# Weight parts at shifted starts in their buffers, and eleven raw tiles in place of twelve, in a one-core fp32 decoder layer

## Chip, cores and metric

The kernel runs on one core of a Trainium2 chip. The metric is the device time of one execution in microseconds (us). Three runs of the kernel before took 1511.15 to 1511.68 us, median 1511.59 us.

## The reference

One conditioned decoder layer on 256 tokens of width 2048, all in fp32, and a final norm:

```python
mod = silu(c) @ w_ada + b_ada          # shift1, scale1, gate1, shift2, scale2, gate2
h   = rms_norm(x, g1) * (1 + scale1) + shift1
p   = h @ w_in                         # retention q,k,v,g | HGRN2 q,f,i,g | gate A | gate B
yA  = (LN_head(retention(rope(q), rope(k), v)) * silu(g)) @ w_ret_o
yB  = (RMS_head(hgrn2(silu(q), f, i)) * silu(g)) @ w_hg_o
x   = x + gate1 * ((sigmoid(gA) * yA + sigmoid(gB) * yB) @ w_out)
h2  = rms_norm(x, g2) * (1 + scale2) + shift2
a,b = split(causal_conv3(h2 @ w_up))   # 2 x 5632 columns
x   = x + gate2 * ((silu(a) * b) @ w_down)
out = rms_norm(x, g_final)
```

What costs is the weights: w_ada (2048 x 12288), w_in (2048 x 12288), w_up (2048 x 11264), w_down (5632 x 2048), and three smaller ones. Each is read once.

## The kernel before

Every large product is made of three products of parts. A weight w is split into a high part wh (w rounded to float32r, the form in which TensorE takes fp32 data in one pass) and a low part wl = w - wh; an activation likewise into a high and a low half, which lie side by side in one block (columns 0 to T and T to 2T, T = 256). The sum is hi x wh + lo x wh + hi x wl.

The weights come in groups of 512 output columns (G). `pieces` walks a group two k-tiles (2 x 128 rows of the weight) at a time. For each such piece `load` starts one transfer of 512 KB from SyncE's queue (SP) into a raw tile, `upper` has ScalarE copy raw into wh (line L169), and `rest` has VectorE subtract wh from raw into wl (L174). Raw has 12 slots, wh and wl 4 each, all in the pool `wp`. A slot of raw is sized for the largest user, the 1025 columns of the modulation dots (`ada_dot`), which stream w_ada through the same raw tiles and reduce it on VectorE (L458). Behind `wp` in SBUF lies the pool `sb`, with the activations in blocks of 4096 bytes (tag k4).

`products` and `up_group` consume the pieces. There are two orientations:

- `mm_rows` (L198, L199 with wh, L203 with wl): the activation is stationary and the weight part is the moving operand, 512 columns wide. It serves part of the input projection, the gates A and B (wab, 8 groups), w_hg_o (whg, 4), w_ret_o (wret, 4), w_out (wout, 4) and w_down (wdown, 4 groups of 44 k-tiles).
- `mm_cols` (L214, L215, L218), `wide_group` with `mm_wide` (L225, L228; the retention q and k, wk, 4 groups) and `up_group` (L1125, L1127; w_up, 22 groups): the weight part is stationary, 128 columns at a time, and the activation moves, 256 or 512 columns wide.

The stages follow each other: norm and modulation with the first stage of the input projection (wa), wk, wab, whg, wret, wout, then the up-projection with its convolution, then w_down and the final norm. Attention work and the modulation of later stages are woven in by `pump`, which runs generators against a budget per piece. Weight loads and conversions are held in program order by `pin` while `self.ordered` is set; elsewhere a scheduler orders them. In the last group of wout and of wdown the weights are multiplied by the gate first (L165). SP's queue is in order, so a load that waits for a free raw slot holds back those behind it.

Of the kernel before, what the change touches and what calls it, by code (L numbers as in the profile page):

```python
# [12 lines left out]
F32 = mybir.dt.float32  # L13
F32R = mybir.dt.float32r
# [5 lines left out]
P = 128  # L20
# [3 lines left out]
KT = D // P  # L24
# [4 lines left out]
FT = FF // P  # L29
G = 512  # L30
# [5 lines left out]
LAG = 1  # L36
NOSYNC = mybir.DependencyInfo(mybir.DependencyClass.NoSync, mybir.DependencyReason.DATA)
SMALL = 70

C_RQ, C_RK, C_RV, C_RG, C_HQ, C_HF, C_HI, C_HG = (i * W1 for i in range(8))  # L40
C_GA, C_GB = 8 * W1, 8 * W1 + D
# [16 lines left out]
class Kernel:  # L58
# [95 lines left out]

    def load(self, src, m, w):
        self.n += 1
        raw = self.wp.tile([P, m, w], F32, name=f"raw_{self.n}", tag="raw", bufs=12)
        self.pin(self.nc.sync.dma_start(out=raw, in_=src))
        return raw

    def upper(self, src, m, w, gain=None):

        raw = self.load(src, m, w)
        if gain is not None:
            self.pin(self.nc.vector.tensor_tensor(raw, raw, gain[:, None, :].to_broadcast([P, m, w]), ALU.mult))  # L165
        self.n += 1
        wh = self.wp.tile([P, m, w], F32R, name=f"wh_{self.n}", tag="wh", bufs=4)
        wl = self.wp.tile([P, m, w], F32R, name=f"wl_{self.n}", tag="wl", bufs=4)
        self.pin(self.nc.scalar.activation(wh, raw, AF.Copy))  # L169
        return raw, wh, wl  # L170

# [3 lines left out]
        self.pin(self.last)  # L175
        return wh, wl

    def pieces(self, src, kts, gain=None):

        uppers = []  # L180
        for k in range(0, kts, 2):
            m = min(2, kts - k)

            while len(uppers) <= k // 2 + (gain is not None) and 2 * len(uppers) < kts:
                at = 2 * len(uppers)
                z = min(2, kts - at)
                uppers.append(self.upper(src[:, at : at + z, :], z, G, gain))
            wh, wl = self.rest(uppers[k // 2])
            uppers[k // 2] = None
            yield [(k + j, wh[:, j, :], wl[:, j, :]) for j in range(m)]  # L190
# [36 lines left out]
            for z in (pair, pair + 1):  # L227
                nc.tensor.matmul(ps[z][:, :T], lhsT=wl[:, z * P : (z + 1) * P], rhs=act[:, :T], start=False, stop=last and i == len(items) - 1)  # L228

    def wide_group(self, src, act):  # L230

        nc = self.nc
        pgs = [self.pg(), self.pg()]
        ps = pgs[0][:2] + pgs[1][:2]
        steps = list(range(0, KT, 4))
        pieces = self.pieces(src, KT)
        for k in steps:
            items = [(act(kt), wh, wl) for _ in range(2) for kt, wh, wl in next(pieces)]
            for pair in (0, 2):
                self.mm_wide(ps, items, k == 0, k == steps[-1], pair)  # L240
                self.pump()
        out = self.blk([P, 4, T], name="p")
        for pair in (0, 2):
            dst = out[:, pair : pair + 2, :]
            z = pgs[pair // 2][2]
            nc.scalar.activation(dst, z[:, :, T:], AF.Copy)
            nc.vector.tensor_tensor(dst, dst, z[:, :, :T], ALU.add)  # L247
        return out

    def products(self, mm, ps, src, act, k0, kts, hold=0, first=True, last=True, gain=None):  # L250

        held = []
        for step in self.pieces(src[:, k0 : k0 + kts, :], kts, gain):
            items = [(act(k0 + kt), wh, wl) for kt, wh, wl in step]
            kt = step[0][0]
            if kt >= kts - hold:
                held += items
            else:
                mm(ps, items, first and kt == 0, last and kt + len(step) == kts)
            self.pump(len(step) / 2)  # L260
        for t in range(NT if held else 0):
            mm(ps, held, hold == kts, True, [t])
        return ps

    def rows(self, src, act, k0=0, kts=KT, ps=None):
        return self.parts(self.products(self.mm_rows, ps or self.pg(), src, act, k0, kts), True)

    def put_split(self, dst, src):

# [524 lines left out]
    def run(self):  # L794
        nc, a = self.nc, self.a
# [42 lines left out]
        ps = [self.po2(), self.po2(), self.pg(), self.pg()][:FIRST]  # L838
# [33 lines left out]
        g = FIRST  # L872
        att, gates = [], {}

        def begin(kind, hb, *ins):
            att.append(self.start(kind(hb, *ins, gates)))
# [43 lines left out]
        self.pace(1, 68.0, 96)  # L920
        sgb, sga = [], []
        for hb in range(2):
            begin(self.retention, hb, *[self.wide_group(a["wk"][2 * hb + i], act) for i in range(2)], v.pop(0))

        og = [[], []]

# [5 lines left out]
        att.append(self.start(gating(1)))  # L932
        for j in range(8):
            gt = self.blk([P, NT, G], name="gt")
            for at, z in self.rows(a["wab"][j], act):
                nc.scalar.activation(gt[:, at, :], z, AF.Sigmoid)
            (sgb if j < 4 else sga).append(gt)
        hT = None
        self.finish(*att)
        self.pace(1, 44.0, 60)  # L940
        for j in range(4):
            for at, z in self.rows(a["whg"][j], lambda k: og[0][k // 2][:, k % 2, :], 0, 8):
                nc.vector.tensor_tensor(sgb[j][:, at, :], sgb[j][:, at, :], z, ALU.mult)
        og[0] = None
        mT = []
# [9 lines left out]
        self.pace(0, 10.0, 16)  # L955
        merges = []
        for j in range(4):
            for at, z in self.rows(a["wret"][j], lambda k: og[1][k // 2][:, k % 2, :], 0, 8):
                nc.vector.tensor_tensor(sga[j][:, at, :], sga[j][:, at, :], z, ALU.mult)
            nc.vector.tensor_tensor(sga[j], sga[j], sgb[j], ALU.add)  # L960
            merges.append(self.start(merged(sga[j])))
# [13 lines left out]
        for j in range(4):  # L975
            last = j == 3
            x1.append(self.load_rows(j))
            if not last:
                g = self.row(self.gate["gate1"], j, "g1")
            if j == 2:  # L980
                g3 = self.row(self.gate["gate1"], 3, "g1")
            elif last:
                g = g3
            ps = self.products(self.mm_rows, self.po2() if last else self.pg(), a["wout"][j], actm, 0, KT, hold=4 * last, gain=g if last else None)
            if last:
                g = None
                self.finish(ada2)
                up = self.pieces(a["wup"][0], KT)
                up = chain([next(up), next(up)], up)
                self.ordered = True  # L990
            if last:
                break
            for t in range(NT):
                self.residual(x1[j], ps, g, ss, j, t)
            if j == 2:
                part = self.row_part(ss)
# [61 lines left out]
        for i in range(FT // 2):  # L1058
            if i == 2:
                g2 = self.start(self.gate_cols("gate2"), 1)  # L1060
                self.pace(1, 38.0, 144)
            if i % 2 == 0:
                gT.append(self.blk([P, 4, T], name="gT"))
            self.up_group(i, act2, gT, up if i == 0 else self.pieces(a["wup"][i], KT), pu if i == 0 else None)
        h2T = None
        self.down(gT, x1, g2)

# [80 lines left out]
    def down(self, gT, x1, g2):  # L1148
        nc, a = self.nc, self.a
        gs = []  # L1150
        sqs = []

        def act(kt):
            if kt == 2 * len(gs):
                z = self.blk([P, 2, 2 * T], F32R, name="gs")
                self.put_split(z, gT[kt // 4][:, kt % 4 : kt % 4 + 2, :])
                gs.append(z)
            return gs[kt // 2][:, kt % 2, :]

        self.finish(g2)  # L1160
        self.gate_row("gate2")
        self.sqrt_table()
        ss = self.small([P, NT, 4], name="ss", bufs=2)
        for j in range(4):
            last = j == 3
            if not last:
                g = self.row(self.gate["gate2"], j, "g2")
            if j == 2:
                g3 = self.row(self.gate["gate2"], 3, "g2")
            elif last:  # L1170
                g = g3
            f = self.row(a["gf"], j, "gf")
            ps = self.products(self.mm_rows, (self.pg, self.po2)[j % 2](), a["wdown"][j], act, 0, FT, hold=8 * last, gain=g if last else None)
            if last:
                g = None
            if j == 0:
                gT = None
            if last:
                self.ordered = True
            for t in range(NT):  # L1180
                self.residual(x1[j], ps, g, ss, j, t)
                if last:

                    y = self.s2([P, G], name="y")
                    self.pin(nc.vector.tensor_tensor(y, x1[j][:, t, :], f, ALU.mult))
                    self.finished([z[:, t, :] for z in x1[:3]] + [y], self.row_rstd(ss, part, t), t)
                else:
                    self.pin(nc.vector.tensor_tensor(x1[j][:, t, :], x1[j][:, t, :], f, ALU.mult))
            if j == 2:
                part = self.row_part(ss)  # L1190
# [101 lines left out]
```

## Time and profile before

| | |
|---|---|
| median of three runs | 1511.59 us |
| the profiled execution | 1511.24 us |
| its span, first to last instruction | 1509.5 us |
| TensorE matmuls | 1493.7 us busy, 8466 |
| weight loads (beside the matmuls) | 1275.5 us |
| VectorE | 1211.9 us |
| ScalarE | 841.7 us |
| read from HBM | 382.11 MB, 255 GB/s over the span |

Busy is the time in which at least one instruction of the engine ran. PE is TensorE's matmuls, PEld its weight loads, DVE VectorE, ACT ScalarE, SP the queue that starts the transfers; an engine name with q is its sequencer, which waits and issues. Matmuls are pipelined: the length of one in the trace is longer than the distance to the next, and the distance is what a stream of them costs. "<-" names what ended a wait.

### The profile page before, as it was taken

How to read it: one execution, taken by the hardware profiler on the slowest of the kernel's cores; microseconds unless marked ns; L12 is line 12 of the kernel's file. 1: busy time of each engine (PE TensorE's matmuls, PEld its weight loads, DVE VectorE, ACT ScalarE, POOL GpSimd, SP SyncE). 2: the span in 40 equal slices, each digit the busy share in tenths (PEclk: the TensorE clock that was granted, in tenths of full speed). 3: DMA queues.
4: the chain of work that ended last, by engine and by line, in shares of the span. 5: the costliest groups of instructions: out<-in, count | busy, mean ns of one | idle time of the engine just before them, and what ended most of it. 6: DMA issues, size and time to landing. Idle time of an engine off the chain costs nothing.

```text
span 1509.5 us, 22703 instructions
## 1 busy us (share of the span) xinstructions
PE 1493.7 (99%) x8466; PEld 1275.5 (84%) x8466; DVE 1211.9 (80%) x1647; ACT 841.7 (56%) x1210; POOL 4.0 (0%) x8
## 2 busy tenths in 40 slices
PE   8999999999999999999999999999999999999997
PEld 6889899888888888888888888888888888888886
DVE  7899997998999877898977778777777769455784
ACT  6745456767775644455466555555555658344342
POOL 0000000000000000000000000000000000000000
PEclk9999999999999999999999999999999999999999
DMA  9999997777887899989847777777777666667651
GB/s 373 376 347 336 321 320 257 265 248 274 281 278 262 285 302 326 318 290 361 298 132 242 229 233 230 230 231 238 229 239 231 216 193 204 197 206 212 183 171 56
DMA packets 110994, 385.71 MB, mean 256 GB/s; under 512 B 12802, under 2 KB 13346, under 8 KB 110884
## 3 DMA queue, kind: packets, MB, share of 16 engines
q1 hardware_dynamic: 110016, 383.14, 76.7%
q8 instruction: 66, 1.08, 0.3%
q10 hardware_dynamic: 868, 1.13, 0.2%
q14 instruction: 44, 0.36, 0.1%
HBM read 382.11 MB, written 2.11 MB: 255 GB/s over the span
## 4 chain that ended last, share of the span: by engine, by line
PE 93%; DVE 3%; ACT 1%; issue 1%; DMA 1%; SPq 0%; DVEq 0%; ACTq 0%
PE pg L198 13%; PE pg L203 13%; PE pg L199 13%; PE po L1125 11%; PE pg L1125 10%; PE po L1127 5%; PE pg L1127 5%; PE pg L225 4%; PE po L198 3%; PE po L203 3%; PE po L199 3%; PE pg L228 2%; DVE wl L174 1%; DVE raw L458 1%; PE po L218 1%
## 5 line engine op out<-in xcount | busy, mean ns | idle before, releaser
L174 DVE TENSOR_TENSOR wl<-raw,wh 128x1024 fp32r<-128x1024 f32 (+1 forms) x536 | 633.1, 1191 | 233.6 <-ACT wh L169 230.6
L169 ACT ACTIVATE wh<-raw 128x1024 fp32r<-128x1024 f32 (+1 forms) x536 | 547.9, 1033 | 482.5 <-PE pg L199 167.0
L458 DVE SCALAR_TENSOR_TENSOR raw<-raw,sc 128x1024 f32<-128x1024 f32 x192 | 233.8, 1222 | 0.1
L1125 PE MATMUL po<-h2T,wh 128*128 128x512 f32 x704 | 221.1, 395 | 0.0
L1125 PE MATMUL pg<-h2T,wh 128*128 128x512 f32 x688 | 216.4, 396 | 0.0
L198 PE MATMUL pg<-wh,hT 128*128 128x512 f32 x512 | 202.1, 395 | 0.9 <-DVE p L830 0.6
L199 PE MATMUL pg<-wh,hT 128*128 128x512 f32 x512 | 199.8, 390 | 0.0
L1127 PEld LDWEIGHTS po<-h2T,wl 128*128 128x128 f32 x704 | 132.3, 188 | 31.3
L1127 PEld LDWEIGHTS pg<-h2T,wl 128*128 128x128 f32 x688 | 129.2, 188 | 31.0 <-DVE wl L174 0.5
L203 PE MATMUL pg<-wl,hT 128*128 128x512 f32 x512 | 138.4, 390 | 0.1
L1127 PE MATMUL po<-h2T,wl 128*128 128x256 f32 x704 | 138.3, 278 | 0.0
L1127 PE MATMUL pg<-h2T,wl 128*128 128x256 f32 x688 | 135.3, 278 | 0.1
L198 PEld LDWEIGHTS pg<-wh,hT 128*128 128x128 f32 x512 | 96.1, 188 | 21.3 <-ACT f L579 1.0
L203 PEld LDWEIGHTS pg<-wl,hT 128*128 128x128 f32 x512 | 96.0, 188 | 20.6 <-DVE wl L174 0.4
L199 PEld LDWEIGHTS pg<-wh,hT 128*128 128x128 f32 x512 | 96.2, 188 | 19.6 <-DVE hT L387 0.3
L1125 PEld LDWEIGHTS po<-h2T,wh 128*128 128x128 f32 x704 | 107.2, 189 | 0.0
L1125 PEld LDWEIGHTS pg<-h2T,wh 128*128 128x128 f32 x688 | 104.7, 189 | 0.0
L199 PE MATMUL pg<-wh,gs 128*128 128x512 f32 x176 | 68.6, 390 | 0.0
L198 PE MATMUL pg<-wh,gs 128*128 128x512 f32 x176 | 68.5, 389 | 0.0
L198 PE MATMUL po<-wh,gs 128*128 128x512 f32 x176 | 68.5, 389 | 0.0
L199 PE MATMUL po<-wh,gs 128*128 128x512 f32 x176 | 68.5, 389 | 0.0
L225 PE MATMUL pg<-hT,wh 128*128 128x512 f32 x256 | 65.1, 396 | 0.2 <-DVE p L247 0.2
(255 smaller groups left out, 2023.3 us busy)
## 6 DMA issues: line engine op xcount, KB each, us to landing
raw<-in_wup SPq DMA_DIRECT2D x176, 512.0 KB, 4.5
raw<-in_wdown SPq DMA_DIRECT2D x88, 512.0 KB, 4.2
raw<-in_wa SPq DMA_DIRECT2D x80, 512.0 KB, 5.7
raw<-in_ada SPq DMA_DIRECT2D x64, 512.5 KB, 5.4
raw<-in_ada SPq DMA_DIRECT2D x64, 512.0 KB, 5.5
raw<-in_wab SPq DMA_DIRECT2D x64, 512.0 KB, 5.0
raw<-in_gate SPq DMA_DIRECT2D x32, 512.5 KB, 4.3
raw<-in_wk SPq DMA_DIRECT2D x32, 512.0 KB, 5.1
```

What stands on the lines that cost most here:

```text
L169: self.pin(self.nc.scalar.activation(wh, raw, AF.Copy))
L174: self.last = self.nc.vector.tensor_tensor(wl, raw, wh.bitcast(F32), ALU.subtract)
L198: nc.tensor.matmul(ps[t], lhsT=act[:, hi], rhs=wh, start=first and i == 0, stop=False)
L199: nc.tensor.matmul(ps[t], lhsT=act[:, lo], rhs=wh, start=False, stop=False)
L203: nc.tensor.matmul(ps[t], lhsT=act[:, hi], rhs=wl, start=False, stop=last and i == len(items) - 1)
L218: nc.tensor.matmul(outs[j], lhsT=wl[:, cs[j]], rhs=act[:, :T], start=False, stop=last and i == len(items) - 1, skip_group_check=True)
L225: nc.tensor.matmul(ps[z], lhsT=wh[:, z * P : (z + 1) * P], rhs=act, start=first and i == 0, stop=False)
L228: nc.tensor.matmul(ps[z][:, :T], lhsT=wl[:, z * P : (z + 1) * P], rhs=act[:, :T], start=False, stop=last and i == len(items) - 1)
L458: dot = self.pin(nc.vector.scalar_tensor_tensor(raw[:, 0, :], raw[:, 0, :], 1.0, self.sc[:, u * GW : u * GW + w], ALU.mult, ALU.mult, accu ...
L1125: self.pin(nc.tensor.matmul(ps[j + z], lhsT=wh[:, cs[z]], rhs=act, start=kt == 0, stop=False, skip_group_check=bool(begun)))
L1127: nc.tensor.matmul(ps[j + z][:, :T], lhsT=wl[:, cs[z]], rhs=act[:, :T], start=False, stop=kt == KT - 1, skip_group_check=bool(begun))
```

## The change

Each group gets a shift, in bytes, from a table. The buffers of wh and wl grow from 1024 to 1152 floats, and the part begins at the group's shift inside its buffer. The groups of the first stage (wa) keep shift 0. Raw has 11 slots instead of 12.

```diff
+SHIFTS = (0, 16, 32, 48, 64, 96, 128, 160, 192, 224, 256, 288, 320, 352, 384, 416, 448, 480, 8, 80, 112, 144, 208, 272)
...
-        raw = self.wp.tile([P, m, w], F32, name=f"raw_{self.n}", tag="raw", bufs=12)
+        raw = self.wp.tile([P, m, w], F32, name=f"raw_{self.n}", tag="raw", bufs=11)
...
+    def part(self, name, m, w, shift):
+
+        full = self.wp.tile([P, 2 * G + P], F32R, name=f"{name}_{self.n}", tag=name, bufs=4)
+        return full[:, shift // 4 : shift // 4 + m * w].rearrange("p (m w) -> p m w", m=m)
+
-    def upper(self, src, m, w, gain=None):
+    def upper(self, src, m, w, gain=None, shift=0):
...
-        wh = self.wp.tile([P, m, w], F32R, name=f"wh_{self.n}", tag="wh", bufs=4)
-        wl = self.wp.tile([P, m, w], F32R, name=f"wl_{self.n}", tag="wl", bufs=4)
+        wh, wl = self.part("wh", m, w, shift), self.part("wl", m, w, shift)
```

`pieces`, `wide_group`, `products` and `rows` pass the shift on. The groups take these entries of the table:

```diff
+  wk:    self.wide_group(a["wk"][2 * hb + i], act, SHIFTS[4 + 2 * (2 * hb + i)])
+  wab:   self.rows(a["wab"][j], act, shift=SHIFTS[j])
+  whg:   ... shift=SHIFTS[8 + j]
+  wret:  ... shift=SHIFTS[12 + j]
+  wout:  ... shift=SHIFTS[16 + j]
+  wup:   self.pieces(a["wup"][i], KT, shift=SHIFTS[i])
+  wdown: ... shift=SHIFTS[20 + j]
```

More of the change, by code (lines that the diff above doesn't have):

```diff
@@ L176, in rest, with pieces @@
         return wh, wl
-    def pieces(self, src, kts, gain=None):
+    def pieces(self, src, kts, gain=None, shift=0):
         uppers = []
@@ L186, in pieces @@
                 z = min(2, kts - at)
-                uppers.append(self.upper(src[:, at : at + z, :], z, G, gain))
+                uppers.append(self.upper(src[:, at : at + z, :], z, G, gain, shift))
             wh, wl = self.rest(uppers[k // 2])
@@ L228, in mm_wide, with wide_group @@
                 nc.tensor.matmul(ps[z][:, :T], lhsT=wl[:, z * P : (z + 1) * P], rhs=act[:, :T], start=False, stop=last and i == len(items) - 1)
-    def wide_group(self, src, act):
+    def wide_group(self, src, act, shift=0):
         nc = self.nc
@@ L235, in wide_group @@
         steps = list(range(0, KT, 4))
-        pieces = self.pieces(src, KT)
+        pieces = self.pieces(src, KT, shift=shift)
         for k in steps:
@@ L248, in wide_group, with products @@
         return out
-    def products(self, mm, ps, src, act, k0, kts, hold=0, first=True, last=True, gain=None):
+    def products(self, mm, ps, src, act, k0, kts, hold=0, first=True, last=True, gain=None, shift=0):
         held = []
-        for step in self.pieces(src[:, k0 : k0 + kts, :], kts, gain):
+        for step in self.pieces(src[:, k0 : k0 + kts, :], kts, gain, shift):
             items = [(act(k0 + kt), wh, wl) for kt, wh, wl in step]
@@ L263, in products, with rows @@
         return ps
-    def rows(self, src, act, k0=0, kts=KT, ps=None):
-        return self.parts(self.products(self.mm_rows, ps or self.pg(), src, act, k0, kts), True)
+    def rows(self, src, act, k0=0, kts=KT, ps=None, shift=0):
+        return self.parts(self.products(self.mm_rows, ps or self.pg(), src, act, k0, kts, shift=shift), True)
     def put_split(self, dst, src):
@@ L922, in run @@
         for hb in range(2):
-            begin(self.retention, hb, *[self.wide_group(a["wk"][2 * hb + i], act) for i in range(2)], v.pop(0))
+            begin(self.retention, hb, *[self.wide_group(a["wk"][2 * hb + i], act, SHIFTS[4 + 2 * (2 * hb + i)]) for i in range(2)], v.pop(0))
         og = [[], []]
@@ L934, in run @@
             gt = self.blk([P, NT, G], name="gt")
-            for at, z in self.rows(a["wab"][j], act):
+            for at, z in self.rows(a["wab"][j], act, shift=SHIFTS[j]):
                 nc.scalar.activation(gt[:, at, :], z, AF.Sigmoid)
@@ L941, in run @@
         for j in range(4):
-            for at, z in self.rows(a["whg"][j], lambda k: og[0][k // 2][:, k % 2, :], 0, 8):
+            for at, z in self.rows(a["whg"][j], lambda k: og[0][k // 2][:, k % 2, :], 0, 8, shift=SHIFTS[8 + j]):
                 nc.vector.tensor_tensor(sgb[j][:, at, :], sgb[j][:, at, :], z, ALU.mult)
@@ L957, in run @@
         for j in range(4):
-            for at, z in self.rows(a["wret"][j], lambda k: og[1][k // 2][:, k % 2, :], 0, 8):
+            for at, z in self.rows(a["wret"][j], lambda k: og[1][k // 2][:, k % 2, :], 0, 8, shift=SHIFTS[12 + j]):
                 nc.vector.tensor_tensor(sga[j][:, at, :], sga[j][:, at, :], z, ALU.mult)
@@ L983, in run @@
                 g = g3
-            ps = self.products(self.mm_rows, self.po2() if last else self.pg(), a["wout"][j], actm, 0, KT, hold=4 * last, gain=g if last else None)
+            ps = self.products(self.mm_rows, self.po2() if last else self.pg(), a["wout"][j], actm, 0, KT, hold=4 * last, gain=g if last else None, shift=SHIFTS[16 + j])
             if last:
@@ L987, in run @@
                 self.finish(ada2)
-                up = self.pieces(a["wup"][0], KT)
+                up = self.pieces(a["wup"][0], KT, shift=SHIFTS[0])
                 up = chain([next(up), next(up)], up)
@@ L1063, in run @@
                 gT.append(self.blk([P, 4, T], name="gT"))
-            self.up_group(i, act2, gT, up if i == 0 else self.pieces(a["wup"][i], KT), pu if i == 0 else None)
+            self.up_group(i, act2, gT, up if i == 0 else self.pieces(a["wup"][i], KT, shift=SHIFTS[i]), pu if i == 0 else None)
         h2T = None
@@ L1172, in down @@
             f = self.row(a["gf"], j, "gf")
-            ps = self.products(self.mm_rows, (self.pg, self.po2)[j % 2](), a["wdown"][j], act, 0, FT, hold=8 * last, gain=g if last else None)
+            ps = self.products(self.mm_rows, (self.pg, self.po2)[j % 2](), a["wdown"][j], act, 0, FT, hold=8 * last, gain=g if last else None, shift=SHIFTS[20 + j])
             if last:
```

## The prediction

> **What bounds the kernel now.** I read the page first (engines, slices, chain), then the windows by stage, then the order of time of a few microseconds, then the waits.
>
> ```profile
> PE 1493.7 (99%) x8466; PEld 1275.5 (84%) x8466; DVE 1211.9 (80%) x1647; ACT 841.7 (56%) x1210; POOL 4.0 (0%) x8
> ...
> PEclk9999999999999999999999999999999999999999
> ...
> PE 93%; DVE 3%; ACT 1%; issue 1%; DMA 1%; SPq 0%; DVEq 0%; ACTq 0%
> ```
>
> TensorE is without work for 1509.5 - 1493.7 = 15.8 us only, and the chain that ended last is TensorE for 93%. The clock is full in every slice. So the time is the number of matmuls times their spacing, plus the idle time at both ends. By stage:
>
> ```profile
> core 0: us, PE busy (x) PEld busy (x) DVE busy (x) ACT busy (x) POOL busy (x), PEclk, DMA share, GB/s
> 0.00:50.00 50.00, 43.85 (x199) 35.06 (x200) 40.07 (x69) 32.53 (x52) 0.21 (x4) 1.00 0.99 382
> 50.00:250.00 200.00, 199.93 (x1133) 176.24 (x1133) 185.60 (x242) 106.66 (x155) 1.91 (x2) 1.00 0.94 330
> 250.00:800.00 550.00, 548.18 (x3427) 462.93 (x3425) 476.54 (x641) 331.25 (x478) 1.91 (x2) 1.00 0.82 279
> 800.00:1250.00 450.00, 450.00 (x2585) 392.66 (x2584) 341.29 (x513) 253.51 (x385) 0.00 (x0) 1.00 0.72 226
> 1494.00:1509.00 15.00, 7.78 (x35) 6.11 (x33) 5.64 (x12) 3.48 (x8) 0.00 (x0) 0.83 0.38 140
> ```
>
> 6.1 us of the idle time lie in the first 50 us, where the DMA engines are full (0.99), 7.2 us in the last 15 us. Between, TensorE never stops, though VectorE is at 77 to 93% and DMA at up to 0.94. A change moves the time if it alters the spacing of matmuls, or makes some supplier late.
>
> **The spacing.** Two lines in order of time, x4 and x8 being merged runs (start, length, engine):
>
> ```profile
> 1340.23 1.07 PE L203 MATMUL po<-wl,gs 128*128 128x512 f32 x4
> 1341.14 0.39 PE L198 MATMUL po<-wh,gs 128*128 128x512 f32 x1
> 202.94 1.12 PE L218 MATMUL pg<-hT,wl 128*128 128x256 f32 x8
> 203.90 0.28 PE L214 MATMUL pg<-hT,wh 128*128 128x256 f32 x1
> ```
>
> One of 512 columns follows the last after (1341.14 - 1340.23) / 4 = 0.227 us, one of 256 after (203.90 - 202.94) / 8 = 0.120 us. The difference of 256 columns is 0.107 us, so each matmul has a fixed part of about 0.120 - 0.107 = 0.013 us whatever its width. In the up-projection a pair (512 and 256 wide) takes 2 x 450.00 / 2585 = 0.348 us, against 0.227 + 0.120 = 0.347.
>
> **The change, part by part.**
>
> *Where the bytes lie.* A raw slot takes 4128 bytes of a partition (1025 floats, rounded up to 32), wh and wl slots 4096 before and 4608 after. The pool of weights takes 12 x 4128 + 8 x 4096 = 82,304 bytes before and 11 x 4128 + 8 x 4608 = 82,272 after. Before, raw begins at 17,440, so wh, wl and every activation block behind them begin 32 bytes beyond a multiple of 128. After, they begin at a multiple of 128, and wh and wl at the group's shift beyond that. So the change is wider than its words: in every fp32r matmul the activation moves by 32 bytes, and the weights' part by the shift (0 in the first stage). Counted from the loops (a group of 512 columns has 96 matmuls in wab and wout, 48 in whg and wret, 128 in wk and wup, 264 in wdown), 5,696 of the 7,472 fp32r matmuls have a shift other than 0: wk 512, wab 672, whg and wret 192 each, wout 384, wup 2688, wdown 1056.
>
> *What an offset costs TensorE.* Matmuls on other addresses are the nearest rows. In the program before, ident and xs lie at multiples of 128, gt, oh and or 32 beyond; p and at lie 32 beyond and a at a multiple. L547 and L408 are the same transpose with the stationary tile at 32 and at 0; L711 and L713 the same product with it at 32 and at 0 (the columns are ns min/median/max).
>
> ```profile
> L547 PEld LDWEIGHTS po<-ident,gt x32: 138/140/143, 646.7 to 686.1; 128*128 128x128 f32 x32
> L547 PE MATMUL po<-ident,gt x32: 270/272/305, 646.9 to 686.2; 128*128 128x128 f32 x32
> L408 PEld LDWEIGHTS po<-ident,xs x20: 137/140/142, 774.5 to 785.0; 128*128 128x128 f32 x20
> L408 PE MATMUL po<-ident,xs x20: 270/272/273, 774.6 to 785.1; 128*128 128x128 f32 x20
> L711 PE MATMUL po<-p,at x32: 270/275/275, 354.8 to 449.9; 128*128 128x128 f32 x32
> L713 PE MATMUL po<-p,a x16: 275/275/275, 358.7 to 450.1; 128*128 128x128 f32 x16
> L1104 PE MATMUL pg<-h2T,wh x32: 278/283/385, 767.4 to 773.5; 128*128 128x256 f32 x32
> L1108 PE MATMUL pg<-h2T,wl x16: 283/283/283, 771.7 to 774.5; 128*128 128x256 f32 x16
> ```
>
> 140 and 140, 272 and 272, 275 and 275: 32 bytes more or less change neither the weight load nor the matmul. L1104 reads its 256 moving columns as two runs of 128, L1108 as one; both take 283 ns, so a second odd start inside the stream costs nothing either. These are only offsets of 0 and 32 and, but for the last two, plain fp32. For the others there is no row; the price is bounded by the fixed part: at best all 13 ns go, at worst another 13 come. I take 0, because every row that differs in address is nearest to it.
>
> *What an offset costs ScalarE and VectorE.* Raw slots are 4128 apart, so their starts run through 0, 32, 64 and 96 of 128, and one group of conversions covers them all:
>
> ```profile
> L169 ACT ACTIVATE wh<-raw x162: 1053/1061/1067, 800.2 to 1248.2; 128x1024 fp32r<-128x1024 f32 x162
> L174 DVE TENSOR_TENSOR wl<-raw,wh x162: 1214/1225/1229, 801.3 to 1249.2; 128x1024 fp32r<-128x1024 f32 x162
> L1139 DVE SCALAR_TENSOR_TENSOR u<-uy,convw,u x88: 474/479/487, 796.2 to 1271.3; 128x255 f32<-128x255 f32 x88
> L1140 DVE SCALAR_TENSOR_TENSOR u<-uy,convw,u x88: 473/479/484, 796.9 to 1272.8; 128x254 f32<-128x254 f32 x88
> L174 DVE TENSOR_TENSOR wl<-raw,wh 128x1024 fp32r<-128x1024 f32 x504 | 613.0, 1223 | 232.4 <-ACT wh L169 230.4 <-ACT sqh L717 1.1
> L174 DVE TENSOR_TENSOR wl<-raw,wh 128x512 fp32r<-128x512 f32 x32 | 21.5, 685 | 1.3 <-PE po L218 1.1 <-ACT wh L169 0.2
> ```
>
> 14 and 15 ns between least and most, so multiples of 32 are free. Starts 4 and 8 bytes off (u from column 1 in L1139, column 2 in L1140) take the same 479 ns. From L174's two sizes a column costs (1223 - 685) / 512 = 1.05 ns and the rest 147, so 255 columns should take 415: the 64 ns above that are the most an odd start can cost here, 0.25 ns a column, 257 ns on a conversion. I take 0. Were it 257, the 162 conversions of 800 to 1250 us would add 41.6 us to VectorE's 341.3 of 450, still below TensorE; that spare time hides it, and with no spare each would delay TensorE by its 257 ns.
>
> *Eleven raw slots.* 536 conversions and 192 dots are 728 loads, one each 1509.5 / 728 = 2.07 us, so a slot comes round after 24.9 us with twelve and 22.8 with eleven. Behind each waiting load on SP's queue stand the later loads and the few row loads; the conversions wait for them.
>
> ```profile
> raw<-in_wa SPq DMA_DIRECT2D x80, 512.0 KB, 5.7
> ...
> SPq L158 <- DVE wl L174: 866.5, 491, 7.1
> SPq L158 <- DVE raw L458: 180.5, 159, 4.3
> SPq L158 <- DMA raw<-in_ada: 13.5, 16, 1.4
> SPq L158 <- DMA raw<-in_wa: 11.2, 20, 2.0
> SPq L158 <- DVE wl L174: 1.6, 4, 0.7
> ACT wh L169 <- PE pg L199: 167.0, 121, 2.6
> ```
>
> Over the span SP waits for slots (866.5 and 180.5 us), so each load will start about one interval later. The need is 5.7 us to landing plus 1.06 and 1.22 for the conversion, 8.0 of 22.8 us: 14.8 stay spare. ScalarE waiting 167 us for TensorE to free wh shows the same: conversions run ahead as far as four buffers allow. The rows of 13.5, 11.2 and 1.6 us are SP's waits of the first 50 us alone, where TensorE does wait for data: there earlier transfers hold SP back (24.7 us), hardly the slots (1.6). Between nothing and one transfer (512 KB at 382 GB/s, 1.4 us) can be lost there; I take 0.4, near nothing, as the 1.6 us say. No instruction is added or removed.
>
> **Sum.** The profiled execution ran 1511.24 us, its span 1509.5. Offsets 0, slots +0.4: 1511.6. The median of the runs is 1511.59, 0.35 above that execution, so 1512.0 for a median.
>
> **The rivals.** A measurement of this kernel tells some 0.2%, 3.0 us, from no change.
>
> *A, faster: the fixed part comes from where the two reads lie.* Before, the moving and the stationary operand of every fp32r matmul begin at the same place of 512 bytes, and no row shows another case. If that makes the two reads collide, the 5,696 shifted matmuls lose up to 13.3 ns: 75.8 us, 1436; a tenth of it gives 1504. It decides from 3.0 us / 5,696 = 0.53 ns each. Against it: L711 reads both at the same place of 512, L713 at 32 apart, and both take 275 ns (plain fp32, though). The Trainium skill's page "TensorE: Matmul & The Clock Gate", section "Wait — 56ns, not 53.3ns?", gives about 2.5 ns for the fixed part of a warm matmul; by it an estimated 10.8 ns of each could go, 61.5 us in all. The trace disagrees with that figure today (13 ns). Its page "SBUF — State Buffer", section "Who interferes with whom", says that the two read ports of TensorE are independent, and by it rival A gains nothing; no run here shows that yet.
>
> *B, slower: TensorE reads starts off a multiple of 32 bytes worse.* Shifts of 8, 16, 48, 80, 112, 144, 208 and 272 are such: 192 matmuls of wab, 192 of wout, 768 of wup, 1056 of wdown, 2,208 in all. At half the fixed part, 6.7 ns, that is 14.7 us: 1526. It decides from 1.4 ns each. No row speaks for it but the fixed part that exists; no fp32r row speaks against it.
>
> *C, slower: eleven slots starve TensorE.* If supply from 50 to 250 us (DMA 0.94) fell by one twelfth, 200 us would become 217: 1528. Against it: landing takes 5.7 us of the 24.9 of a slot, so under a quarter of the slots is in transit. It decides once the spare 14.8 us are gone.
>
> **How the numbers follow.** Forecast, no change that can be told: 0.63, own range 1508.6 to 1514.6. A 0.17, B 0.13, C 0.07. So faster 0.17, same 0.63, slower 0.20. The range takes the forecast and the nearer half of A and B: 1500 to 1522, about 0.82.
>
> **What would show it.** Right: L203 in wab and wdown still every 0.227 us in each group, the up-projection at 0.348 us a pair for all 22 groups, L174 near 1225 ns in every group, TensorE idle within 1 us of 15.8. Wrong by A or B: spacing that steps at the borders of groups. Wrong by C: TensorE idle between 50 and 1494 us, ended by a transfer or by wl. A gain in the first stage, where the shift is 0, would be the 32 bytes of the activations.

## The result, and the profile after

The changed kernel took 1525.17 us (median of three runs, 1524.83 to 1525.31) against 1511.59 before: 13.6 us slower, ratio 1.009 with a 95% interval of 1.0067 to 1.0113. The prediction of 1512.0, range 1500 to 1522, was wrong. The profiled execution took 1525.31 us.

The page after, and the windows by stage (PE is busy time and, in brackets, matmuls that touch the window):

```profile
span 1523.5 us, 22700 instructions
...
PE 1507.5 (99%) x8466; PEld 1278.4 (84%) x8466; DVE 1212.6 (80%) x1647; ACT 841.6 (55%) x1210; POOL 4.0 (0%) x8
...
PEclk9999999999999999999999999999999999999999
```
```profile
0.00:50.00 50.00, 43.53 (x197) 34.80 (x198) 39.53 (x69) 32.74 (x52) 0.20 (x4) 1.00 0.99 379
50.00:250.00 200.00, 199.93 (x1132) 176.15 (x1131) 185.76 (x242) 106.05 (x154) 1.91 (x2) 1.00 0.93 327
250.00:800.00 550.00, 548.21 (x3389) 457.20 (x3388) 472.30 (x636) 326.11 (x469) 1.91 (x2) 1.00 0.81 274
800.00:1250.00 450.00, 450.00 (x2580) 393.31 (x2579) 338.59 (x507) 252.44 (x381) 0.00 (x0) 1.00 0.72 228
```

TensorE is busy 13.8 us longer with the same 8466 matmuls at the same full clock, and idle 16.0 us against 15.8. VectorE and ScalarE have the same busy time. So nothing is late: the matmuls themselves stand further apart. In the first 250 us, where the shift is 0, as many are done as before (1132 against 1133 from 50 to 250 us); between 250 and 800 us 38 fewer.

In order of time, two groups of w_down, first the one with shift 112, then the one with 144:

```profile
1300.14 1.07 PE L208 MATMUL pg<-wl,gs 128*128 128x512 f32 x4
1301.05 0.39 PE L203 MATMUL pg<-wh,gs 128*128 128x512 f32 x1
...
1349.63 1.10 PE L208 MATMUL po<-wl,gs 128*128 128x512 f32 x4
1350.56 0.39 PE L203 MATMUL po<-wh,gs 128*128 128x512 f32 x1
```

The first four follow each other after (1301.05 - 1300.14) / 4 = 0.228 us as before, the second after 0.233. The column of the mean length of one hides this: it is 393 to 395 ns for w_down's wide ones against 389 to 390 before, since a modelled end is part of it. Distances between starts have to be read.

Taken from the starts in the trace, by shift (mean distance in ns, those that hold a wait left out; the pair is a 512- and a 256-wide one of the up-projection):

```text
shift                   0     8    16    32    48    64    80    96   112   128   144   160   192   208   224   256
weights move (512)  227.1 233.5 231.5 233.4 233.1 229.3 231.2 233.4 226.8 232.4 233.3 234.3 233.3 234.7 233.3 227.2
up-projection pair  348.3 349.9 353.3 351.3 346.7 346.7 351.3 351.7 351.7 348.9 351.6 350.7 345.2    -  346.8 348.6
```

(The 0 of the up-projection is the kernel before.) Summed over all float32r matmuls, start to start, those with moving weights took 12.3 us more, the up-projection 1.4 more, the rest nothing: 13.7 of the 13.8 us. The values at 288, 320, 352, 384, 416, 448 and 480 repeat those at 32 to 224 within 0.4 ns in both rows, so in this kernel what counts repeats every 256 bytes.

### The profile page after: what moved, and what is told of

Its sections match the earlier page's. It is cut to its first block, busy times and chain, and to the rows that moved or that the text cites. A ratio compares the mean times of both kernels' runs of the same rounds, so it can differ in the third digit from the quotient of the medians.

```text
span 1523.5 us, 22700 instructions
## 1 busy us (share of the span) xinstructions
PE 1507.5 (99%) x8466; PEld 1278.4 (84%) x8466; DVE 1212.6 (80%) x1647; ACT 841.6 (55%) x1210; POOL 4.0 (0%) x8
## 4 chain that ended last, share of the span: by engine, by line
PE 95%; DVE 2%; DMA 1%; ACT 1%; issue 1%; SPq 0%; ACTq 0%; DVEq 0%
PE pg L203 13%; PE pg L208 13%; PE pg L204 13%; PE po L1130 11%; PE pg L1130 10%; PE po L1132 5%; PE pg L1132 5%; PE pg L230 4%; PE po L204 3%; PE po L208 3%; PE po L203 3%; PE pg L233 2%; PE po L219 1%; PE po L220 1%; PE po L223 1%; PE pg L220 1%
```

## The experiments

Three theories were put to the test. R: a matmul is slowed by the distance between the starts of its two operands, moving and stationary, counted modulo 256 bytes. A: it is slowed by where the weights' part starts, whatever the other operand does. S: the loss comes from the eleven slots.

**All shifts 0, eleven slots.**

```diff
-SHIFTS = (0, 16, 32, 48, ...)
+SHIFTS = (0,) * 24
```

> All shifts 0, buffers still 1152 floats, eleven raw slots: the change without its shifts. Theory R (a matmul is slowed by the distance between the start of its moving and of its stationary operand, counted modulo 256 bytes): the distance is 0 as before, so TensorE busy 1493 to 1495 us and 1511 to 1513 us in all. Theory A (slowed by where the weights' part itself starts): the parts start at 128 of 256 instead of 160, so a time other than 1511.6 is possible; in the changed kernel's first stage, which has shift 0, nothing moved, so also about 1512. Theory S (eleven slots): 1525, with TensorE busy 1493.7 and the loss as idle time.

It took 1511.69 us against 1511.82 of the kernel before in the same session, ratio 0.9999 (0.9989 to 1.0008). Neither the twelfth slot nor the larger buffers nor the move of both operands by 32 bytes shows in the time; theory S falls.

**Only the activations move.** The kernel before, 32 bytes in front of the pool `sb`:

```diff
+        gap = ctx.enter_context(tc.tile_pool(name="gap", bufs=1))
+        self.nc.vector.memset(gap.tile([P, 8], F32, name="gap"), 0.0)
         self.sb = ctx.enter_context(tc.tile_pool(name="sb", bufs=1))
```

> The kernel before, with 32 bytes put in front of the pool of activations; the weights' parts and the raw slots stay where they were, twelve raw slots. Theory R: the distance becomes that of a shift of 224 (minus 32). In the changed kernel matmuls with 512 moving weight columns were 6.7 ns further apart at that shift, the up-projection's pair 1.3 ns closer: 3360 x 6.7 = +22.5 us, 1408 x 1.3 = -1.8 us, 1530 to 1534 us in all. Theory A: no weight part has moved, 1511 to 1513 us. Theory S: 1511 to 1513 us.

1536.71 us, ratio 1.0164 (1.0149 to 1.0179), above the 1530 to 1534 of theory R. No weight was touched, and it is slower than the change itself. Its page, and one line of w_down and one of the first stage in order of time:

```profile
PE 1518.5 (99%) x8466; PEld 1276.4 (83%) x8466; DVE 1213.9 (79%) x1648; ACT 841.4 (55%) x1210; POOL 4.0 (0%) x8
```
```profile
1402.47 1.09 PE L205 MATMUL po<-wl,gs 128*128 128x512 f32 x4
1403.40 0.40 PE L200 MATMUL pg<-wh,gs 128*128 128x512 f32 x1
...
201.76 1.10 PE L220 MATMUL pg<-hT,wl 128*128 128x256 f32 x8
202.69 0.28 PE L216 MATMUL pg<-hT,wh 128*128 128x256 f32 x1
```

TensorE is busy 24.8 us longer. Matmuls with moving weights are at 0.233 us, as at shift 224, and cost 20.2 us in sum; the narrow ones of the first stage are at (202.69 - 201.76) / 8 = 0.116, faster than the 0.120 before (2.2 us won). Theory A falls. What R had wrong is the up-projection: its pair took 353.3 ns, not the 346.8 of shift 224, 6.7 us lost in place of 1.8 won.

**Both operands move together.** Shift 96 in every group, and 96 bytes in front of `sb`:

```diff
-SHIFTS = (0, 16, 32, 48, ...)
+SHIFTS = (96,) * 24
...
-    def upper(self, src, m, w, gain=None, shift=0):
+    def upper(self, src, m, w, gain=None, shift=96):
...
+        gap = ctx.enter_context(tc.tile_pool(name="gap", bufs=1))
+        self.nc.vector.memset(gap.tile([P, 24], F32, name="gap"), 0.0)
```

> Every weights' part at shift 96 and 96 bytes in front of the pool of activations, so both operands of every float32r matmul move together; eleven raw slots. Theory R: the distance is 0, so 1511 to 1513 us. Theory A: what shift 96 cost in the changed kernel, 7 ns on each of 3360 matmuls with moving weights: 1533 to 1537 us. Theory S: 1525 us.

1511.30 us, ratio 0.9996 (0.9986 to 1.0006); w_down reads as in the kernel before:

```profile
1401.07 1.07 PE L210 MATMUL pg<-wl,gs 128*128 128x512 f32 x4
1401.98 0.39 PE L205 MATMUL pg<-wh,gs 128*128 128x512 f32 x1
```

(1401.98 - 1401.07) / 4 = 0.228 us. With the first run and the kernel before, both operands have now begun at 128, 160 and 224 of 256 bytes, always together, and always in the same time. So the loss comes from the distance of the two.

**The up-projection at the best shift.**

```diff
-            self.up_group(i, act2, gT, up if i == 0 else self.pieces(a["wup"][i], KT, shift=SHIFTS[i]), pu if i == 0 else None)
+            self.up_group(i, act2, gT, up if i == 0 else self.pieces(a["wup"][i], KT, shift=192), pu if i == 0 else None)
```

The start of group 0 likewise; all other shifts are 0.

> As the change, but shift 0 in all groups except the up-projection, whose 22 groups all have 192. In the changed kernel the pair of matmuls there took 345.25 ns at shifts 192 and 448 against 348.0 before, the least of all shifts. Theories R and A: 1408 x 2.75 = -3.9 us, 1507 to 1509 us. Theory S: 1521 us.

1507.11 us, ratio 0.9968 (0.9956 to 0.9980), so a distance other than 0 can also win. Its window of the up-projection:

```profile
800.00:1250.00 450.00, 450.00 (x2611) 396.01 (x2610) 345.00 (x520) 258.05 (x392) 0.00 (x0) 1.00 0.72 228
```

2 x 450.00 / 2611 = 0.345 us a pair, where the kernel before had 0.348.

**A second set of shifts.** One run, the change with these:

```diff
+SHIFTS = (24, 40, 56, 72, 88, 104, 120, 136, 152, 168, 176, 184, 200, 216, 232, 240, 248, 368, 116, 108, 4, 12, 60, 20)
+UPS = (24, 40, 56, 72, 88, 104, 120, 136, 152, 168, 176, 184, 188, 196, 200, 208, 216, 232, 240, 248, 4, 12)
+KEYSHIFTS = (192, 224, 48, 160)
+COLSHIFTS = (224, 192, 48, 160)
```

> The change with other shifts: 24, 40, 56, 72, 88, 104, 120, 136, 152, 168, 176, 184, 200, 216, 232, 240, 248, 368, 116, 108, 4, 12, 60, 20 in the 24 groups with moving weights, 22 such values in the up-projection, 192, 224, 48, 160 in wk, and 224, 192, 48, 160 in the four groups of the first stage whose weights are stationary. Theory R (distance of the two reads, period 256 bytes): the group at 368 is spaced 226.5 ns as the one at 112 was, 216 and 232 near 208 and 224 (232 to 235); nearly all others 229 to 235, so slower than before, 1520 to 1535 us. Rival F: 226.5 ns is a floor of matmuls with moving weights, none goes below; if instead 0 is just one good value among many, some new value is below 226. For VectorE my price of at most 257 ns for an odd start is tested by the shifts 4, 12, 20, 60, 108 and 116: subtraction 1225 ns (no price) up to 1480.

1529.06 us against 1512.56 beside it. No group with moving weights went below the 227 ns of distance 0; the nearest were 228.3 at 60, 228.9 at 12 and 229.1 at 108, most lay at 231 to 236, the worst were 239.6 at 116 and 240.0 at 20. So 227 held as a floor. The expectation for 368 did not hold: 231.1, not 227. Since 368 is 112 modulo 256, the distance alone does not fix the spacing. By the starts, the matmuls at 368 stood 225, 231 and 237 to 238 ns apart in turn through the whole group; the group at 112 in the changed kernel also began at 225 to 236, but soon settled at 226 to 227. In the first stage the group at 192 stood at 114.3 ns instead of 120. For the conversions, the groups of w_down, which have the odd starts 4, 12, 60 and 20 here:

```profile
L182 DVE TENSOR_TENSOR wl<-raw,wh x78: 1216/1226/1229, 1284.9 to 1499.6; 128x1024 fp32r<-128x1024 f32 x78
L177 ACT ACTIVATE wh<-raw x77: 1042/1061/1067, 1286.1 to 1498.5; 128x1024 fp32r<-128x1024 f32 x77
```

1226 and 1061 ns: none of these starts costs VectorE or ScalarE anything.

**The same distance at another place.** Place means where the two operands begin modulo 256 bytes. One run each. The first has shifts 0, eleven slots and the 32 bytes in front of `sb` (places 128 and 160); the second puts another 32 bytes in front of `wp`, so that the operands lie at the places (160 and 192 of 256) of the run in which only the activations moved:

```diff
+        front = ctx.enter_context(tc.tile_pool(name="front", bufs=1))
+        self.nc.vector.memset(front.tile([P, 8], F32, name="front"), 0.0)
         self.wp = ctx.enter_context(tc.tile_pool(name="wp", bufs=1))
```

> All shifts 0 with eleven raw slots, and 32 bytes in front of the activations: the distance of the run with 32 bytes in front (minus 32), but both operands begin 32 bytes earlier. If the distance alone decides: the same as there, an up-projection pair of 353.4 ns, matmuls with moving weights 233.3 ns, 1535 to 1538 us. If the place counts too wherever the distance is not 0: another pair, towards the 347 ns that the changed kernel's group at 224 had with both operands 64 bytes earlier, 1527 to 1534 us.

> As the run with 32 bytes in front of the activations and eleven raw slots, but everything from the weights' pool on another 32 bytes later: both operands begin in the same places of 256 bytes as in the run with twelve raw slots, the wh and wl slots stay 4608 apart instead of 4096. If the place decides between the two up-projection pairs seen at distance minus 32 (353.4 and 347.0 ns): 353.4 ns, 1535 to 1538 us. If the pitch of the slots decides: 347.0 ns, 1527 to 1530 us.

1528.21 and 1536.81 us. The window of the up-projection, first without, then with the 32 bytes in front of `wp`:

```profile
800.00:1250.00 450.00, 449.89 (x2596) 396.44 (x2595) 342.17 (x510) 254.76 (x383) 0.00 (x0) 1.00 0.73 230
```
```profile
800.00:1250.00 450.00, 449.89 (x2546) 389.11 (x2545) 338.60 (x506) 250.88 (x379) 0.00 (x0) 1.00 0.72 226
```

Pairs of 0.347 and 0.353 us. Where the distance is not 0 the place counts as well, for the up-projection; matmuls with moving weights were at 233.3 ns in both. This amends R and accounts for its miss above.

**wh and wl at different shifts.** One run:

```diff
-        wh, wl = self.part("wh", m, w, shift), self.part("wl", m, w, shift)
+        wh, wl = self.part("wh", m, w, shift), self.part("wl", m, w, 16 if shift == 192 else shift)
```

The up-projection has shift 192, all else 0.

> All shifts 0 except in the up-projection, where wh lies at 192 (the best shift, wide matmuls 226 to 232 ns) and wl at 16 (among the worst, 234 to 235). The order there is two wide ones with wh, two narrow ones with wl. If a matmul's moving stream is held up by the weight load of the next matmul: the second wide one of each two, whose successor loads wl, is at 234 to 235 ns, the first at 226 to 229. If by its own weight load: both wide ones at 226 to 232. In all 1507 to 1514 us.

1515.61 us, above the expected 1507 to 1514. All four wide matmuls of a k-tile stood at 232 to 233 ns, the narrow ones at 118, so neither pattern appeared. If a weight load is what disturbs the moving stream, whether it is a matmul's own or the next one's is not settled.

**Shift 192 for all stationary weights.** Shift 192 wherever the weights' part is stationary (`COLSHIFTS`, `KEYSHIFTS` and `UPS` all 192), 0 wherever it moves.

> Shift 192 wherever the weights' part is stationary (the first four groups of the first stage, wk, the up-projection), 0 wherever it moves. From the survey's groups at 192: 114.3 ns in place of 120 on 768 matmuls of the first stage (-4.4 us), 229.1 + 115.7 in place of 230.2 + 121.1 on 256 pairs of wk (-1.7 us), and the 4.7 us that the up-projection alone gave. Theory R: 1499 to 1503 us, TensorE busy 1481 to 1484 us. Rival: the first stage is bound by transfers, so that its matmuls' gain turns into idle time: 1503 to 1506 us.

1505.86 us, ratio 0.9960 (0.9946 to 0.9973): faster than both kernels, but not by what was expected. Its page and a line of the first stage:

```profile
PE 1487.9 (99%) x8466; PEld 1273.0 (85%) x8466; DVE 1211.4 (80%) x1647; ACT 841.2 (56%) x1210; POOL 4.0 (0%) x8
```
```profile
200.97 1.10 PE L226 MATMUL pg<-hT,wl 128*128 128x256 f32 x8
201.91 0.28 PE L222 MATMUL pg<-hT,wh 128*128 128x256 f32 x1
```

TensorE's idle time is 17.0 us, 1.2 more than before, so although 1505.86 lies in the range of the rival, a stage bound by transfers takes little of the gain. The up-projection gave its 4.6 us; the first stage gave about 768 x 2.1 ns = 1.6 us in place of 4.4, and wk 0.6 in place of 1.7. The first stage stands at (201.91 - 200.97) / 8 = 0.118 us, by the starts 117.8 ns, not the survey's 114.3 at the same distance and place. The first group of wk in this run, at 192 throughout, has both values side by side:

```profile
291.69 1.07 PE L236 MATMUL pg<-hT,wl 128*128 128x256 f32 x8
292.59 1.99 PE L233 MATMUL pg<-hT,wh 128*128 128x512 f32 x8
294.42 1.11 PE L236 MATMUL pg<-hT,wl 128*128 128x256 f32 x8
295.37 2.00 PE L233 MATMUL pg<-hT,wh 128*128 128x512 f32 x8
```

The first eight narrow ones stand at (292.59 - 291.69) / 8 = 0.113 us, the next eight at (295.37 - 294.42) / 8 = 0.119, and the two values alternate from there on. The two blocks read different columns, 1024 bytes apart, but in the other groups of wk either block can be the faster one. So at 192 a stream of matmuls has more than one steady spacing at the same distance and place, and what ran just before seems to select it. No run tests that, and why the first stage settled at 114 in one kernel and at 118 in the other stays open.

## Why the prediction was wrong

*What bounds the kernel*: right. The time is the number of matmuls times their spacing, and the whole loss lies there.

*What an offset costs TensorE*: this step failed. It took 0, and measured were 12.3 us / 2496 = 4.9 ns on each matmul with moving shifted weights and about 1 ns on a pair of the up-projection, 13.7 us in all. The zero came from L547, L408, L711 and L713, plain fp32 matmuls. With the activations moved by 32 bytes these read as before (L549 and L713 are the L547 and L711 of the kernel before):

```profile
L549 PEld LDWEIGHTS po<-ident,gt x32: 138/141/144, 655.2 to 695.1; 128*128 128x128 f32 x32
L549 PE MATMUL po<-ident,gt x32: 270/272/275, 655.4 to 695.3; 128*128 128x128 f32 x32
L713 PE MATMUL po<-p,at x32: 271/275/276, 357.5 to 453.7; 128*128 128x128 f32 x32
```

In the same run the float32r ones lost 24.7 us in sum (20.2 + 6.7 - 2.2). Only L549 tests the distance here, since p and at moved together; by the starts, its matmuls follow each other after 109 ns at the median in both kernels, so the plain fp32 transposes are indeed indifferent to it. Two more things were wrong with the evidence. Lengths include a modelled end, so a few ns of spacing hardly show in them; and the float32r rows quoted beside them, L1104 and L1108, all have the operands at distance 0, as every float32r matmul of the kernel before has. The prediction named that gap under rival A and still let rows of another kind close it. It also took the weights' parts to move by the shift alone, where by its own addresses they moved by the same 32 bytes as the activations and by the shift on top; that left the distance, and the time, of the first stage unchanged.

*Conversions*: right, 0; the bound of 257 ns was not needed (a median of 1225 ns over all subtractions of 1024 columns before, 1224 after, 1225 with the second set of shifts).

*Eleven slots*: right within 0.5 us; 0.4 was forecast, and 0.13 less than the kernel before was measured, inside its interval. SP's waits for raw slots in the first 50 us did rise, from 1.8 to 7.5 us in the changed kernel, as the step said.

*Rivals.* A had the right variable, the distance of the two reads, and for moving weights the wrong sign: agreeing starts are their best case, so the 13 ns there are not caused by them. For stationary weights A's sign was right at some distances (345.2 in place of 348.3 ns a pair at 192). B came out at the right size (1526 forecast, 1525.2 measured) by luck, with the wrong mechanism: starts off a multiple of 32 are no worse than those on one (112 at 226.8 ns and 80 at 231.2, but 32 at 233.4, 160 at 234.3). No change was given 0.63 although the one row that bears on it, a float32r matmul at another distance, did not exist. C did not occur.

The range ended too early: it took in the nearer half of B only, though no row excluded B, and 1525.2 lies just beyond. The parts it names, 0.63 and half of 0.17 and of 0.13, make a chance of 0.78; the 0.82 needs half of C as well. Two readings were a little off, with nothing resting on them: VectorE from 800 to 1250 us is busy 341.29 of 450 us, 76% and not 77, and TensorE does stop between the ends, for 1.8 us of 250 to 800.

The Trainium skill's page "SBUF — State Buffer", section "Who interferes with whom", says that TensorE's two read ports are independent and that TensorE never waits on anyone. The runs speak against the first: moving one of the two operands by 32 bytes cost 24.9 us, moving both by 96 nothing. That the two reads meet in SBUF is the nearest reading of this, but no run shows it from inside. ScalarE and VectorE are not the ones that are met, as the second says: in the group with shift 144 the spacing was 233 ns at the median whether ScalarE, or VectorE, was busy through the matmul or idle (90 matmuls or more in each of the four cases).

## What to carry over

Where TensorE is the bound with float32r operands, the distance between the starts of the moving and the stationary operand, modulo 256 bytes, is a tuning knob worth -0.4 to +1.6% here; pad buffers as a whole so that it stays 0, and try others only by measurement, for each orientation apart, in the kernel itself, since the same setting settled at different spacings in different surroundings. A change that enlarges one pool moves all that lies behind it, so compare the distances, not only the buffers that the diff names. And rows of another data type say nothing on a few ns of a float32r matmul: the plain fp32 transposes kept their 109 ns where float32r matmuls with moving weights lost 6 ns each.

## What the runs showed that was not expected

- Moving by 32 bytes the tiles that no line of the weights' path touches cost 24.9 us (1536.71 against 1511.82).
- At distance 0 the place did not count (1511.6, 1511.7 and 1511.3 us at three places); elsewhere it did, 0.347 or 0.353 us for the same pair.
- At 192 the same narrow matmuls stood at 113 or 119 ns within one group, with distance and place unchanged.
- Stationary weights gain at 192 (0.345 us a pair), while moving weights have their floor of 227 ns at 0.
